# A two-layer hybrid decoder on one core: other slot counts for the experts, 512-column turns for the small ones, whole-piece splits, rows summed ahead of the transposes

## The chip, the core and the metric

The kernel runs on one core of a Trainium2 chip. The core has five engines, each with an instruction queue of its own that it works through in order: PE (TensorE, matrix products; its weight loads are listed as PEld), DVE (VectorE), ACT (ScalarE), POOL (GpSimd) and SP (SyncE, which here issues the transfers). Sixteen DMA engines move data between HBM and the on-chip memory SBUF. Matrix products are written to PSUM, eight banks of 128 x 512 fp32. The metric is the device time of one execution in microseconds; the kernel before takes 1657.78 us (median of three runs, 1655.46 to 1666.21).

## What is computed

Two decoder layers over 256 tokens of 1024 features, all in float32. Each layer has a mixer with three head groups and then a feed-forward part; layer 0 has a dense SwiGLU, layer 1 a top-2-of-8 expert SwiGLU. The change touches the experts alone. Cut to that:

```python
def moe_swiglu(x, w_router, w1, w3, w2):            # w1, w3: 8 x 1024 x 3584; w2: 8 x 3584 x 1024
    xf = x.reshape(-1, D)                           # 256 tokens
    logits = jnp.einsum('nd,de->ne', xf, w_router)
    top_logits, top_idx = lax.top_k(logits, 2)
    gates = jax.nn.softmax(top_logits, axis=-1)
    ...                                             # each token goes to its two experts only
    def expert_block(args):
        xb, e = args
        h = jax.nn.silu(xb @ w1[e]) * (xb @ w3[e])
        return h @ w2[e]
    ...                                             # times the gate, added over the two experts
```

The 256 tokens make 512 assignments. With the reference's default inputs (seed 0) its router gives the eight experts 72, 21, 20, 180, 51, 52, 32 and 84 of them.

## The kernel before

**Precision.** fp32 products are made of fp32r halves: `split(src, hi, lo)` lets ACT copy the source rounded to `hi` (L174) and DVE write the rest, `lo = src - hi` (L175). `mm3` then makes hi x hi, lo x hi and hi x lo, three matmuls for one.

**Weights.** All expert weights are read, 8 x 3 x 14 MiB, in pieces of 1 MiB: 128 partitions x 2048 fp32. `stage` takes a landing buffer `w` and issues the transfer on SP (L186), alternately from the pools "base" and "more"; `parts` takes a `whi` and a `wlo` buffer of the same pool and splits the piece in two halves of 1024 columns. Per pool there are three `w`, two `whi`, two `wlo` (`WB = (3, 2, 2)`), so six landing buffers and four pairs. A `w` is free when DVE has made its `wlo`, a pair when PE has used it.

**Experts.** Routing, up to about 605 us, ranks the tokens. Expert 0 always is job 0 (its first weights are loaded before the routing is known); the other seven are sorted by the number of their tokens and become jobs 1 to 7. A job has a fixed number of slots: 128 for job 0, 256 for job 1, 128 for jobs 2 to 4, 64 for jobs 5 to 7. `gather` picks a job's tokens by one-hot matmuls into `x` (hi and lo), `scatter` brings results back and adds them to `xt`, by gate. If any job has more tokens than slots, a second pass under `tc.If(over > 128)` at the end does the remainder; it is skipped otherwise.

- `one_by_one` does jobs 0, 2, 3, 4, each in NF = 7 steps of 512 hidden columns. In a step `first` makes x @ w1 and x @ w3 with the 128 slots as the stationary operand and 512 weight columns moving (two pieces each, 12 matmuls a piece, `t<-whi,x`), then SiLU and product, four transposes (L1204), `hT` (hi and lo), and `second` for the step before (two pieces of `w2`, 12 matmuls each, `py<-whi,hT`). One step: six pieces.
- `side_by_side` then does job 1 and jobs 5 to 7 together in 14 steps of 256 hidden columns. For job 1, w1 and w3 are stationary and 256 slots move (`t<-x,whi`, two groups `a` of 48 matmuls), `jT` is the result, and `w2` follows a step later. For the small jobs `mm_packed` makes two matmuls of three: the 64 slots' hi and lo stand side by side as 128 stationary columns (`flat(a)`, L1154 and L1158), the `wlo` term uses the 64 hi columns alone (L1156). Three such 256-column turns follow each step of job 1; the two halves of their result are added (`both`, L1279 ACT, L1280 DVE), then SiLU and product for all three turns (L1296, L1297), six transposes of 64 rows (L1261) and a split into `hT`. One step: three pieces of job 1 and nine of the small jobs.

`chores` is a list of gathers and scatters done in small portions between. PSUM holds two banks `t1` and six banks `py`. The order of instructions on each engine is set before the run by a scheduler that starts from the order of the code and follows each operation's inputs and buffers.

Of the kernel before, what the change touches and what calls it, by code (L numbers as in the profile page):

```python
# [7 lines left out]
F32 = mybir.dt.float32  # L8
F32R = mybir.dt.float32r
# [29 lines left out]
def tile_hybrid_decoder(ctx: ExitStack, tc: tile.TileContext, x_in, w_in, mix_scale, w_out, gdn_conv_w,  # L39
# [10 lines left out]
    wp = {"more": None, "small": None, "n": 0,  # L50
# [138 lines left out]
    def parts(staged):  # L189

        which, w = staged
# [757 lines left out]
    def moe(l):  # L949
        li = l // 2  # L950
        with ExitStack() as es:
# [39 lines left out]
            main = [Job(0, 128), Job(1, 256)] + [Job(k, 128 if k < 5 else 64) for k in range(2, NE)]  # L991
# [26 lines left out]
            slots = gp.tile([128, SEQ], F32, name="slots")  # L1018
            G.iota(slots, pattern=[[1, SEQ]], base=1, channel_multiplier=0, allow_small_or_imprecise_dtypes=True)
# [30 lines left out]
            pair = gp.tile([128, 2, 64], F32, name="pair")  # L1050
            V.tensor_copy(pair, slots[:, None, :64].to_broadcast([128, 2, 64]))
            pair = pair.rearrange("p s t -> p (s t)")
# [21 lines left out]
            def gather(jb, tag, pos=posj):  # L1074

                n, k = jb.n, jb.k
                big = n == 256
                w = min(n, 128)
# [4 lines left out]
                for c in range(n // w):  # L1083
                    oh = gp.tile([128, NB, 128], F32R, name="oh", tag="oh", bufs=2)
                    row = pair if n == 64 else slots[:, jb.base + 128 * c:jb.base + 128 * c + 128]
                    for b in range(NB):
                        V.tensor_scalar(oh[:, b, :], row, pos[:, b, k:k + 1], None, op0=OP.is_equal)
# [9 lines left out]
                    for hf in range(2):  # L1097
# [3 lines left out]
                        cut = x[:, 4 * hf:4 * hf + 4, :, w * c:w * c + w]  # L1101
# [113 lines left out]
            def side_by_side(big, small, pend):  # L1215

                n = FFN_EXPERT // 256
                steps = [(jb, f) for jb in small for f in range(n)]
                late = big_late = None
                for f in range(n + 1):  # L1220
                    now = steps[3 * f:3 * f + 3]
                    if f < n:
                        hT = gp.tile([128, 2, 2, SEQ], F32R, name="jT", tag="hT", bufs=4)
# [3 lines left out]
                        for a in range(2):  # L1227
                            p = bank("t1").rearrange("p (m t) -> p m t", m=2)
# [4 lines left out]
                            h = gp.tile([128, SEQ], F32, name="h", tag="h", bufs=2)  # L1233
                            S.activation(h, p[:, 0, :], AF.Silu)
                            V.tensor_mul(h, h, p[:, 1, :])  # L1235
                            split(h, hT[:, a, 0, :], hT[:, a, 1, :])
                    if f == 0:
                        second(*pend)
                        chores.append((pend[0], scatter(pend[0], "py")))
                        chore()  # L1240
                    else:
# [4 lines left out]
                        for g, y in enumerate(big.y):  # L1246
                            t = slice(128 * g, 128 * g + 128)
                            for hf in range(2):
                                cc = slice(512 * hf, 512 * hf + 512)
                                mm3(y[hf], [((big_late[:, k, 0, t], big_late[:, k, 1, t]), (hi[:, k, cc], lo[:, k, cc]))  # L1250
                                            for k in range(2)], f == 1, f == n, True)
                        if f == n:
                            chores.append((big, scatter(big, "t1")))
                            chore()
                    if f < n:
                        big_late = hT
                    if late:
                        hs, before = late
                        pt = bank("t1")[:, :384].rearrange("p (q t) -> p q t", q=6)
                        for q in range(6):  # L1260
                            T.transpose(pt[:, q, :], hs[:, q // 2, 0, 128 * (q % 2):128 * (q % 2) + 128],  # L1261
                                        ident[:64, :64])
                        sT = gp.tile([128, 6, 2, 64], F32R, name="hT", tag="hT", bufs=4)
                        split(pt, sT[:, :, 0, :], sT[:, :, 1, :])
                    if now:
                        both = gp.tile([64, 3, 2, 256], F32, name="both", tag="both", bufs=1)
                    for i in range(3):
                        if now:
                            jb, fs = now[i]
                            if jb.x is None:  # L1270
                                chores.append((jb, gather(jb, "t1")))
                            ws = [load(jb.rows(w)[:, :, 256 * fs:256 * fs + 256], 8, 256) for w in (moe_w1, moe_w3)]
                            finish(jb)
                            p = bank("t1").rearrange("p (m t) -> p m t", m=2)
                            for m, w in enumerate(ws):
# [129 lines left out]
```

## Time and profile before

| | us |
|---|---|
| median of 3 runs (1655.46 to 1666.21) | 1657.78 |
| the profiled execution: its own time | 1654.85 |
| its span in the trace | 1652.6 |
| `one_by_one`, 605 to 1108 | 503 |
| `side_by_side`, 1108 to 1631 | 523 |
| PE, DVE, ACT busy over the span | 1564.1, 1370.0, 1020.7 |
| moved over the span | 430.03 MB |

Busy times of engines overlap. Matmuls are pipelined and their ends are modelled, so a PE that is "busy" may still have room; the distance between starts of consecutive matmuls says more. A wait is put down to the one that ended last. The bounds of the two stages are the first expert matmul, the first of `side_by_side`'s group `a=0`, and the last matmul of the last `w2` piece.

### The profile page before, as it was taken

How to read it: one execution, taken by the hardware profiler on the slowest of the kernel's cores; microseconds unless marked ns; L12 is line 12 of the kernel's file. 1: busy time of each engine (PE TensorE's matmuls, PEld its weight loads, DVE VectorE, ACT ScalarE, POOL GpSimd, SP SyncE). 2: the span in 40 equal slices, each digit the busy share in tenths (PEclk: the TensorE clock that was granted, in tenths of full speed). 3: DMA queues.
4: the chain of work that ended last, by engine and by line, in shares of the span. 5: the costliest groups of instructions: out<-in, count | busy, mean ns of one | idle time of the engine just before them, and what ended most of it. 6: DMA issues, size and time to landing. Idle time of an engine off the chain costs nothing. (4 is left out here: it accounts for less than half of the span.)

```text
span 1652.6 us, 28180 instructions
## 1 busy us (share of the span) xinstructions
PE 1564.1 (95%) x11147; PEld 1358.0 (82%) x11147; DVE 1370.0 (83%) x1902; ACT 1020.7 (62%) x1375; POOL 66.3 (4%) x82
## 2 busy tenths in 40 slices
PE   7898899998899979999999999999999999999995
PEld 6887699996888768888888888888888889888893
DVE  7987854555898788998989889887998988898997
ACT  5334544442425457777777767766787777777783
POOL 5001100000201100000000000000000000000000
PEclk9999899998899979999999999999999999999998
DMA  5351755532314567999999999997999999999991
GB/s 146 104 165 68 228 197 190 176 114 79 91 53 167 178 230 272 363 366 338 362 342 349 331 345 350 333 343 264 355 364 335 343 324 328 366 323 337 344 372 75
DMA packets 274795, 430.03 MB, mean 260 GB/s; under 512 B 11900, under 2 KB 181938, under 8 KB 274656
## 3 DMA queue, kind: packets, MB, share of 16 engines
q1 hardware_dynamic: 272864, 423.81, 74.4%
q0 software_dynamic: 1792, 4.35, 0.9%
q8 instruction: 89, 1.46, 0.4%
q14 instruction: 50, 0.41, 0.1%
HBM read 427.08 MB, written 1.05 MB: 259 GB/s over the span
## 5 line engine op out<-in xcount | busy, mean ns | idle before, releaser
L175 DVE TENSOR_TENSOR wlo<-w,whi 128x1024 fp32r<-128x1024 f32 (+1 forms) x812 | 938.7, 1203 | 133.7 <-ACT whi L174 126.0
L174 ACT ACTIVATE whi<-w 128x1024 fp32r<-128x1024 f32 (+1 forms) x812 | 792.0, 1037 | 227.1 <-PE py L217 43.2
L215 PE MATMUL t<-whi,x 128*128 128x512 f32 x448 | 179.4, 400 | 0.3 <-DVE x L175 0.3
L217 PE MATMUL t<-whi,x 128*128 128x512 f32 x448 | 176.2, 393 | 0.0
L222 PE MATMUL t<-wlo,x 128*128 128x512 f32 x448 | 124.4, 396 | 0.0
L215 PE MATMUL t<-x,whi 128*128 128x256 f32 x448 | 109.5, 282 | 0.0
L219 PE MATMUL t<-x,whi 128*128 128x256 f32 x448 | 109.4, 282 | 0.0
L215 PE MATMUL pj<-xth,whi 128*128 128x256 f32 x368 | 98.4, 302 | 5.7 <-ACT whi L174 2.5
L215 PEld LDWEIGHTS t<-whi,x 128*128 128x128 f32 x448 | 84.2, 188 | 19.9 <-DVE x L175 0.5
L222 PEld LDWEIGHTS t<-wlo,x 128*128 128x128 f32 x448 | 83.8, 188 | 20.1 <-DVE wlo L175 0.4
L217 PEld LDWEIGHTS t<-whi,x 128*128 128x128 f32 x448 | 84.4, 188 | 18.2
L1154 PE MATMUL t<-whi,x 128*128 128x256 f32 x588 | 87.3, 287 | 8.5 <-DVE x L175 3.3
L219 PE MATMUL pj<-xtl,whi 128*128 128x256 f32 x368 | 94.8, 292 | 0.0
L1156 PE MATMUL t<-wlo,x 128*64 128x256 f32 x672 | 94.5, 282 | 0.0
L1154 PEld LDWEIGHTS t<-whi,x 128*128 128x128 f32 x588 | 78.1, 190 | 14.6 <-DVE h L1235 4.4
L215 PE MATMUL py<-whi,hT 128*128 128x512 f32 x224 | 88.0, 393 | 0.0
L217 PE MATMUL py<-whi,hT 128*128 128x512 f32 x224 | 87.4, 390 | 0.0
L219 PE MATMUL ph<-xtl,whi 128*128 128x256 f32 x352 | 86.9, 285 | 0.0
L215 PE MATMUL ph<-xth,whi 128*128 128x256 f32 x352 | 86.8, 284 | 0.0
L219 PEld LDWEIGHTS t<-x,whi 128*128 128x128 f32 x448 | 84.4, 188 | 0.8
L215 PEld LDWEIGHTS t<-x,whi 128*128 128x128 f32 x448 | 84.4, 188 | 0.7
L1156 PEld LDWEIGHTS t<-wlo,x 128*64 128x64 f32 x672 | 81.8, 136 | 1.8
(426 smaller groups left out, 2792.7 us busy)
## 6 DMA issues: line engine op xcount, KB each, us to landing
w<-in_moe_w_dram SPq DMA_DIRECT2D x333, 1024.0 KB, 6.4
w<-in_ffn_w_dram SPq DMA_DIRECT2D x33, 1024.0 KB, 5.3
w<-in_w_in_dram SPq DMA_DIRECT2D x18, 1024.0 KB, 5.5
w<-in_w_out_dram SPq DMA_DIRECT2D x8, 1024.0 KB, 5.1
w<-in_w_in_dram SPq DMA_DIRECT2D x14, 512.0 KB, 3.8
spare<-in_moe_w_dram SPq DMA_DIRECT2D x3, 1024.0 KB, 5.1
xt<-in_x_dram SPq DMA_DIRECT2D x2, 512.0 KB, 4.1
gam<-in_ln_mix_g_dram POOLq DMA_DIRECT2D x2, 512.0 KB, 4.3
```

The source lines that it names most:

```text
L174: S.activation(hi, src, AF.Copy)
L175: return V.tensor_sub(lo, src, hi.bitcast(F32))
L215: T.matmul(o, a[0], b[0], start=first and i == 0, stop=False)
L217: T.matmul(o, a[1], b[0], start=False, stop=False)
L219: T.matmul(o, a[0], b[1], start=False, stop=False)
L222: m = T.matmul(o, a[0], b[1], start=False, stop=last and i == n - 1)
L1154: T.matmul(o, flat(a), b[0], start=first and i == 0, stop=False)
L1156: T.matmul(o[:64], a[:, 0, :], b[1], start=False, stop=False)
```

## The change

Jobs have 128, 192 and 128 slots for jobs 0, 1, 2, and 64 for jobs 3 to 7. `one_by_one` does jobs 0 and 2 only. `side_by_side` runs two generators in turns: `wide` (job 1, 256-column steps as before, but 192 moving slots, and for `w2` three matmuls for its first 128 slots and two, packed, for its last 64) and `packed` (jobs 3 to 7, one after the other, each in 7 steps of 512 columns; a piece of w1 or w3 has 4 x 512 columns like those of `one_by_one`). In `packed` the two halves of a result, each 64 x 512, are added by ACT and DVE as they come; w1's and w3's sums are then transposed separately, and SiLU and product follow on 128 x 256. `wide` yields after `a=0`, after `a=1` and after `w2` (42 times), `packed` once a step (35 times). In the whole expert layer a piece is split in one ACT and one DVE operation of 2048 columns. The second pass, if it is needed, covers all eight jobs.

```diff
     def parts(staged):
 
+        if wp["whole"]:
+            return whole_parts(staged)
         which, w = staged
...
+    def whole_parts(staged):
+        which, w = staged
+        m = w.shape[1] * w.shape[2]
+        r = []
+        for name, n in (("whi", WB[1]), ("wlo", WB[2])):
+            t = wp[which].tile([128, 2048], F32R, name=name, tag=name, bufs=n)
+            r.append(t[:, :m].rearrange("p (a b) -> p a b", a=w.shape[1]))
+        split(w, *r)
+        return r
...
     def moe(l):
         li = l // 2
+        wp["whole"] = True
...
-            main = [Job(0, 128), Job(1, 256)] + [Job(k, 128 if k < 5 else 64) for k in range(2, NE)]
+            main = [Job(0, 128), Job(1, 192), Job(2, 128)] + [Job(k, 64) for k in range(3, NE)]
...
-            slots = gp.tile([128, SEQ], F32, name="slots")
+            slots = gp.tile([128, SEQ + 64], F32, name="slots")
...
-            pair = gp.tile([128, 2, 64], F32, name="pair")
-            V.tensor_copy(pair, slots[:, None, :64].to_broadcast([128, 2, 64]))
...
+            def packed(jobs, tag):
+
+                pend = None
+
+                def half(jb, w, f):
+
+                    p = bank("t1")
+                    for j, src in zip((0, 4), first_pieces(jb, w, f)):
+                        hi, lo = load(*src)
+                        mm_packed(p, [(jb.x[:, j + q], (hi[:, q, :], lo[:, q, :])) for q in range(4)], j == 0, j == 4)
+                    r = gp.tile([64, 512], F32, name="both", tag="both", bufs=3)
+                    S.activation(r, p[64:], AF.Copy)
+                    V.tensor_add(r, r, p[:64])
+                    return r
+
+                def close(jb, sT, f):
+                    if f == 0:
+                        jb.y = [jb.ys()]
+                    for q, src in zip((0, 2), second_pieces(jb, f)):
+                        hi, lo = load(*src)
+                        for hf in range(2):
+                            cc = slice(512 * hf, 512 * hf + 512)
+                            mm_packed(jb.y[0][hf], [(sT[:, q + k], (hi[:, k, cc], lo[:, k, cc])) for k in range(2)],
+                                      f == 0 and q == 0, f == NF - 1 and q == 2)
...
+                for n, jb in enumerate(jobs):
...
+                    for f in range(NF):
+                        if f == 0:
+                            finish(jb)
+                        hs = [half(jb, moe_w1, f)]
+                        yield
+                        hs.append(half(jb, moe_w3, f))
+                        if pend:
+                            close(*pend)
+                        chore()
+
+                        pt = bank("t1").rearrange("p (m q t) -> p m q t", m=2, q=4)
+                        for m, r in enumerate(hs):
+                            for q in range(4):
+                                T.transpose(pt[:, m, q, :], r[:, 128 * q:128 * q + 128], ident[:64, :64])
+                        h = gp.tile([128, 4, 64], F32, name="h", tag="h", bufs=2)
+                        S.activation(h, pt[:, 0], AF.Silu)
+                        V.tensor_mul(h, h, pt[:, 1])
+                        sT = gp.tile([128, 4, 2, 64], F32R, name="sT", tag="hT", bufs=4)
+                        split(h, sT[:, :, 0, :], sT[:, :, 1, :])
+                        pend = (jb, sT, f)
...
+            def wide(big):
...
+                n, nt = FFN_EXPERT // 256, big.n
+                before = None
                 for f in range(n + 1):
                     if f < n:
+                        hT = gp.tile([128, 2, 2 * nt], F32R, name="jT", tag="hT", bufs=4)
                         ws = [load(big.rows(w)[:, :, 256 * f:256 * f + 256], 8, 256) for w in (moe_w1, moe_w3)]
...
                         for a in range(2):
+                            p = bank("t1")[:, :2 * nt].rearrange("p (m t) -> p m t", m=2)
...
+                            yield
+                    if f > 0:
...
                         hi, lo = load(big.rows(moe_w2)[:, 2 * f - 2:2 * f, :], 2, D)
+                        for hf in range(2):
+                            cc = slice(512 * hf, 512 * hf + 512)
+                            ws = [(hi[:, k, cc], lo[:, k, cc]) for k in range(2)]
+                            mm3(big.y[0][hf], [((before[:, k, :128], before[:, k, 256:]), ws[k]) for k in range(2)],
+                                f == 1, f == n, True)
+                            mm_packed(big.y[1][hf], [(before[:, k, 128:256].rearrange("p (s t) -> p s t", s=2), ws[k])
+                                                     for k in range(2)], f == 1, f == n)
...
+                        yield
                     if f < n:
+                        before = hT
+
+            def side_by_side(big, small, pend):
+
+                a, b = wide(big), packed(small, "t1")
+                na, nb = 3 * (FFN_EXPERT // 256), NF * len(small)
+                done = 0
+                next(a)
+                second(*pend)
...
+                for i, _ in enumerate(b):
+                    while (done + 1) * nb < (i + 1) * na and next(a, "end") != "end":
+                        done += 1
+                for _ in a:
+                    pass
                 chore(100)
...
-            pend = one_by_one([main[k] for k in (0, 2, 3, 4)], [main[1], main[5]])
-            side_by_side(main[1], main[5:], pend)
+            pend = one_by_one([main[k] for k in (0, 2)], [main[1], main[3]])
+            side_by_side(main[1], main[3:], pend)
...
-                pend = one_by_one([Job(k, 128, 128) for k in (0, 2, 3)] + [Job(k, 128, 64) for k in (5, 6, 7)])
+                pend = one_by_one([Job(k, 128, 192 if k == 1 else 128 if k < 3 else 64) for k in range(NE)])
```

Three places show what the change does to the queues. The first is PE, two pieces of w1 of a small job before; `t1` is the PSUM bank, `whi` and `wlo` the weight buffers, `x` the packed slots (numbers tell buffers apart).

```order
L1154 MATMUL t1_12102<-whi_12088,x_10952 128x256 x7
L1156 MATMUL t1_12102<-wlo_12089,x_10952 64x256 x8
L1158 MATMUL t1_12102<-whi_12088,x_10952 128x256
L1154 MATMUL t1_12102<-whi_12096,x_10952 128x256 x7
L1156 MATMUL t1_12102<-wlo_12097,x_10952 64x256 x8
L1158 MATMUL t1_12102<-whi_12096,x_10952 128x256
```

Here the same place now, two pieces of w3 of a small job.

```order
L1167 MATMUL t1_11278<-whi_11281,x_10843 128x512 x3
L1169 MATMUL t1_11278<-wlo_11282,x_10843 64x512 x4
L1171 MATMUL t1_11278<-whi_11281,x_10843 128x512
L1167 MATMUL t1_11278<-whi_11295,x_10843 128x512 x3
L1169 MATMUL t1_11278<-wlo_11296,x_10843 64x512 x4
L1171 MATMUL t1_11278<-whi_11295,x_10843 128x512
```

A piece has moved from 16 matmuls of 256 columns to 8 of 512, and both pieces now belong to one of the two matrices.

The second place is DVE in the middle of `side_by_side` before, from the product of job 1's group `a=0` on; `w` is the landing buffer, `jT` and `hT` the transposed hidden values.

```order
L1235 TENSOR_TENSOR h_12766<-h_12766,t1_12717 128x256
L175 TENSOR_TENSOR wlo_12879<-w_12876,whi_12878 128x1024 x2
L175 TENSOR_TENSOR jT_12700<-h_12766,jT_12700 128x256
L175 TENSOR_TENSOR wlo_12922<-w_12919,whi_12921 128x2x512 x2
L1235 TENSOR_TENSOR h_12820<-h_12820,t1_12771 128x256
L175 TENSOR_TENSOR jT_12700<-h_12820,jT_12700 128x256
```

And ACT now, from the two first pieces of a step of job 1 (`whi_11213`, `whi_11219`) over the six packed pieces that stand between its groups `a=0` (`t1_11223`) and `a=1`; the last of the six, `whi_11384`, follows four rows later.

```order
L174 ACTIVATE whi_11213<-w_11211 128x2048
L174 ACTIVATE whi_11219<-w_11217 128x2048
L1274 ACTIVATE h_11164<-t1_11155 128x256
L174 ACTIVATE sT_11167<-h_11164 128x4x64
L174 ACTIVATE whi_11281<-w_11279 128x2048
L1239 ACTIVATE both_11207<-t1_11175 64x512
L174 ACTIVATE whi_11295<-w_11293 128x2048
L1304 ACTIVATE h_11272<-t1_11223 128x192
L1307 ACTIVATE jT_11210<-h_11272 128x192
L174 ACTIVATE whi_11312<-w_11310 128x2048
L1239 ACTIVATE both_11307<-t1_11278 64x512
L174 ACTIVATE whi_11326<-w_11324 128x2048
```

Before, a piece was two rows of 1024 columns, and between job 1's two products stood its own splits, the last pieces of a small job and the coming `w2`; now a piece is one row of 2048, and a small job's next pieces stand between job 1's two groups.

The third place is PE at the end of those six pieces, where `a=1` begins (`t1_11399`), on the buffers that `a=0` used.

```order
L1167 MATMUL t1_11367<-whi_11384,x_10843 128x512 x3
L1169 MATMUL t1_11367<-wlo_11385,x_10843 64x512 x4
L1171 MATMUL t1_11367<-whi_11384,x_10843 128x512
L227 MATMUL t1_11399<-x_8193,whi_11213 128x192
L231 MATMUL t1_11399<-x_8193,whi_11213 128x192
```

The second use of `whi_11213` stands behind six packed pieces, where the groups of job 1 followed each other before.

## Rows read from the trace of the kernel before

**Rows 1.** The page, part 1: busy time, share of the span, instructions of each engine.

```profile
PE 1564.1 (95%) x11147; PEld 1358.0 (82%) x11147; DVE 1370.0 (83%) x1902; ACT 1020.7 (62%) x1375; POOL 66.3 (4%) x82
```

**Rows 2.** Busy time by stretch; the columns stand in the first line.

```profile
core 0: us, PE busy (x) PEld busy (x) DVE busy (x) ACT busy (x) POOL busy (x), PEclk, DMA share, GB/s
605.00:1108.00 503.00, 501.29 (x2277) 409.41 (x2278) 445.39 (x443) 368.98 (x415) 0.00 (x0) 1.00 0.94 339
1108.00:1631.00 523.00, 506.77 (x3496) 451.34 (x3496) 464.36 (x494) 392.35 (x481) 1.10 (x2) 0.99 0.96 329
700.00:1080.00 380.00, 380.00 (x1710) 309.75 (x1709) 334.73 (x328) 277.63 (x315) 0.00 (x0) 1.00 0.96 347
1140.00:1600.00 460.00, 448.61 (x3140) 401.46 (x3140) 410.23 (x432) 348.00 (x424) 1.10 (x2) 1.00 1.00 341
```

**Rows 3.** Waits from 700 to 1100 us: total, times, longest; ACT's, then SP's.

```profile
ACT whi L174 <- PE t L217: 24.7, 35, 2.4
...
SPq L186 <- DVE wlo L175: 316.5, 131, 5.2
```

**Rows 4.** Timeline of ACT in stage A: start, length, what.

```profile
690.97 0.58 ACT L174 ACTIVATE hT<-t 128x512 fp32r<-128x512 f32 x1
...
708.02 0.58 ACT L174 ACTIVATE hT<-t 128x512 fp32r<-128x512 f32 x1
```

**Rows 5.** Timeline of PE: start, length (of xN: of the whole run), what.

```profile
801.39 1.03 PE L1100 MATMUL py<-ident,xs 128*128 128x128 f32 x8
...
1104.84 0.28 PE L215 MATMUL t<-x,whi 128*128 128x256 f32 x1
1104.96 0.28 PE L219 MATMUL t<-x,whi 128*128 128x256 f32 x1
...
1113.63 0.40 PE L217 MATMUL py<-whi,hT 128*128 128x512 f32 x1
1113.86 0.40 PE L215 MATMUL py<-whi,hT 128*128 128x512 f32 x1
...
1302.14 0.58 PE L1261 MATMUL t<-ident,both 64*128 64x64 f32 x6
...
1309.19 1.10 PE L1156 MATMUL t<-wlo,x 128*64 128x256 f32 x8
```

**Rows 6.** Groups by line and form, 720 to 1652: busy, mean ns, idle before.

```profile
L175 DVE TENSOR_TENSOR wlo<-w,whi 128x1024 fp32r<-128x1024 f32 x590 | 687.2, 1215 | 69.8 <-ACT whi L174 64.0 <-PE t L224 5.4
L174 ACT ACTIVATE whi<-w 128x1024 fp32r<-128x1024 f32 x588 | 579.8, 1051 | 106.7 <-PE t L219 24.3 <-PE t L217 21.6 <-PE t L1158 21.0
...
L1280 DVE TENSOR_TENSOR both<-both,t 64x512 f32<-64x512 f32 x42 | 28.2, 672 | 0.4 <-ACT both L1279 0.4
...
L175 DVE TENSOR_TENSOR hT<-t,hT 128x512 fp32r<-128x512 f32 x22 | 15.0, 683 | 2.5 <-ACT hT L174 2.5
...
L1204 PE MATMUL t<-ident,h 128*128 128x128 f32 x88 | 13.2, 272 | 0.0
...
L175 DVE TENSOR_TENSOR jT<-h,jT 128x256 fp32r<-128x256 f32 x28 | 11.7, 418 | 3.9 <-ACT jT L174 3.9
```

**Rows 7.** Busy time in two stretches of 10 us; columns as in rows 2.

```profile
610.00:620.00 10.00, 8.34 (x39) 6.53 (x38) 10.00 (x14) 8.28 (x9) 0.00 (x0) 1.00 1.02 394
...
1220.00:1230.00 10.00, 10.00 (x74) 9.14 (x74) 8.15 (x10) 7.93 (x11) 0.00 (x0) 1.00 1.07 368
```

**Rows 8.** Timeline of DVE in `side_by_side`: start, length of the run, what.

```profile
1308.86 6.89 DVE L175 TENSOR_TENSOR wlo<-w,whi 128x1024 fp32r<-128x1024 f32 x6
```

**Rows 9.** Stretches of 2 us where `side_by_side` begins; columns as in rows 2.

```profile
1124.00:1126.00 2.00, 0.00 (x0) 0.00 (x0) 2.00 (x4) 0.00 (x0) 0.00 (x0) 0.79 0.28 107
1126.00:1128.00 2.00, 1.78 (x8) 1.78 (x9) 0.17 (x1) 0.00 (x0) 0.00 (x0) 0.50 0.49 132
...
1130.00:1132.00 2.00, 2.00 (x12) 2.00 (x11) 1.72 (x2) 1.19 (x2) 0.00 (x0) 0.51 0.07 23
```

**Rows 10.** Timeline of PE there: start, length, what, idle before and its releaser.

```profile
1126.22 1.01 PE L1154 MATMUL t<-whi,x 128*128 128x256 f32 x3 [2.90 <-DVE x L175]
```

More of the change, by code (lines that the diff above doesn't have):

```diff
@@ L48, in tile_hybrid_decoder @@
     mcst = mixers.enter_context(tc.tile_pool(name="mcst", bufs=1, reuse_waits="tile"))
-    wp = {"more": None, "small": None, "n": 0,
+    wp = {"more": None, "small": None, "n": 0, "whole": False,
           "base": ctx.enter_context(tc.tile_pool(name="wgt", bufs=1, side="right", reuse_waits="tile"))}
@@ L1082, in gather @@
                 jb.ohT = []
[L1083 removed]
+                for c in range(0, n, 128):
+                    w = min(n - c, 128)
                     oh = gp.tile([128, NB, 128], F32R, name="oh", tag="oh", bufs=2)
[L1085 removed]
                     for b in range(NB):
[L1087 removed]
+                        dst, row = oh[:, b, :], slots[:, jb.base + c:jb.base + c + w]
+                        if w == 64:
+                            dst, row = dst.rearrange("p (s t) -> p s t", s=2), row[:, None, :].to_broadcast([128, 2, 64])
+                        V.tensor_scalar(dst, row, pos[:, b, k:k + 1], None, op0=OP.is_equal)
                     xs = [gp.tile([128, 512], F32, name="xs", tag="h", bufs=2) for hf in range(2)]
@@ L1212, in one_by_one @@
                 return pend
[L1215 to L1219, printed above, removed]
+            def packed(jobs, tag):
[18 more added lines that the diff above has]
+                                      f == 0 and q == 0, f == NF - 1 and q == 2)
+                    if f == NF - 1:
+                        chores.append((jb, scatter(jb, tag)))
+                        chore()
+                for n, jb in enumerate(jobs):
+                    if jb.x is None:
+                        chores.append((jb, gather(jb, tag)))
+                    for f in range(NF):
[6 more added lines that the diff above has]
+                            close(*pend)
+                        chore()
+                        pt = bank("t1").rearrange("p (m q t) -> p m q t", m=2, q=4)
[8 more added lines that the diff above has]
+                        pend = (jb, sT, f)
+                        if f == NF - 3 and n + 1 < len(jobs):
+                            chores.append((jobs[n + 1], gather(jobs[n + 1], tag)))
+                        chore()
+                close(*pend)
@@ L1295, in side_by_side @@
-                    if now:
-                        S.activation(both[:, :, 0, :], both[:, :, 0, :], AF.Silu)
-                        V.tensor_mul(both[:, :, 0, :], both[:, :, 0, :], both[:, :, 1, :])
-                        late = (both, now)
-                        for jb, _ in steps[3 * f + 3:3 * f + 9]:
-                            if jb.x is None and not any(jb is c[0] for c in chores):
-                                chores.append((jb, gather(jb, "t1")))
+                        before = hT
```

73 lines of the change are left out of this document (13 added, 60 removed).

## The prediction

> **What bounds the kernel now.** The page first [rows 1]: TensorE is busy 95% of the span, VectorE 83%, so averages settle nothing and the expert layer has to be read by stage. It has two [rows 2]: A, `one_by_one` (605 to 1108 us, four experts of 128 slots, 28 steps of 512 hidden columns), and B, `side_by_side` (1108 to 1631, 14 steps, each one big and three small 256-column steps). Weights come in pieces of 1 MiB, 168 per stage; ACT makes `whi`, DVE `wlo`, PE uses both.
>
> In stage A the waits [rows 3] show ACT waiting for PE to give `whi` buffers back and SP waiting for DVE to free a landing buffer; no engine waits for a transfer. One step, from one `hT` to the next without gather or scatter, takes 708.02 - 690.97 = 17.05 us [rows 4]. PE's starts stand 0.23 us apart with 512 columns and 0.12 with 256 [rows 5]; 72 matmuls x 0.23 plus four transposes are 17.0. So A is exactly PE. In B a step needs 192 x 0.117 + 48 x 0.23 + 0.6 = 34.1 us of PE (0.117 = (1.10 - 0.28) / 7, the run of eight); 14 steps are 477, with 25 for gathers and scatters 502 of the 523 us. B is PE-bound to 96%, with the transfers close behind: share 1.07 at 368 GB/s in a dense spell [rows 7].
>
> **The change part by part.** The sum is made against the profiled execution's 1654.85 us (span 1652.6 and 2.2 around it), 0.2% under the median of the runs.
>
> *Two experts leave stage A.* 14 of 28 steps go, 14 x 17.05 = 239 us, with half of the 503 - 477 = 26 us for gathers and scatters: A loses 251 and keeps 252.
>
> *Stage B becomes 252 pieces*: 35 packed steps (five experts of 64 slots x 7, six pieces each) and 14 wide steps (192 slots, three pieces). I sum it per resource, for none is hidden behind the others by a margin.
>
> PE. A packed piece is 8 matmuls of 512 columns instead of 12: 1.84 us. A packed step is 6 x 1.84 + 0.7 (eight 64-column transposes; six last 0.58) = 11.7; 35 are 411. A wide step has 96 matmuls of 192 columns and 20 of 512. No row has 192 columns. Scaled from 256 they would take 0.088; if loading 128 weight columns sets the pace they stay at 0.117; a run of eight 128-column transposes, 0.27 us each [rows 6], has (1.03 - 0.27) / 7 = 0.108, though only half as many columns move, so I take 0.11. A wide step is then 10.6 + 4.6 = 15.2 (13.0 to 15.8), 14 are 212 (182 to 221). With 30 for gathers and scatters PE needs 653 (623 to 662).
>
> DVE. A split of 1024 columns lasts 1.215 us, one of 512 0.683 [rows 6]: 1.04 ns a column, so 2.28 for 2048. Queued, a run of six takes 6.89 [rows 8], so each overlaps its neighbour by 0.08: two halves 2.29, a whole piece 2.21. 252 pieces are 557. The rest, by the same rows less 0.07 each: 35 x 1.9 for a packed step (two adds, one product, one subtraction), 14 x 1.3 for a wide one, 34 for scatters and gathers: 119. DVE needs 676; in stage B before it was busy 464 of 523, 89% [rows 2].
>
> Transfers. 252 pieces are 264.2 MB. Stage A's plain step moves 6.29 MB in 17.05 us, 369 GB/s, with 512- and 1024-column rows, which most of B now also has. At that rate B takes 716 us. Bounds: 394, a dense stretch of 10 us [rows 7], 671; 347 and 341, the averages of most of A and of B with their stops [rows 2], 761 and 775. The Trainium skill (DMA: Bandwidth & Descriptors, "Where 436 GB/s comes from") says that the HBM side binds a load from HBM at about 358 GB/s. By that B would take 738, a step of A 17.6, and the sum would be 1627. The trace does not agree: A holds 369.
>
> ACT needs less: 1.051 for 1024 columns [rows 6], so about 1.9 for 2048, 252 x 1.9 + 125 = 604.
>
> *A wait the change adds.* There are four `whi`/`wlo` pairs, two per pool. A wide step now takes its two first pieces, does `a=0`, then one packed step (six pieces) stands in PE's queue ahead of `a=1`, which still needs both. So six pieces pass through two pairs. One pair's round is 1.9 (ACT) + 2.28 (DVE) + 1.15 (the five matmuls after `wlo` arrives) + 0.1 = 5.4 us, 2.7 per piece, where DVE alone would need 2.2: 3.0 us over six pieces. During `a=0` and `a=1` (5.3 us each) DVE can fill only two pairs, 4.4: 2 us more. While DVE waits, its adds and products behind the blocked `wlo` wait too, and PE for them. Before, with halves, DVE could start after 1.05, a round was 4.6, and no other expert's first pieces stood between the two groups. DVE's other work fills part of the 5 us: 0 to 5 us x 14, so DVE with holds is 676 to 746; I take the middle, 711.
>
> Transfers (716) and DVE (711) are thus equally high and share six landing buffers, so what one loses the other cannot make up. Stage B before ran 4% over its highest sum (523 against 502); I take 2.5% over 716: **735**.
>
> *Nothing*: the wider `slots` on POOL and one DVE operation more against two `pair` copies ahead of the routing are under 1 us. The repeat pass under `over > 128` is not entered: the reference's router, on its default inputs, gives the experts 72, 21, 20, 180, 51, 52, 32 and 84 assignments, which fit 128 / 192 / 128 / 64. What follows 1631 us (last scatter, LayerNorm) stays.
>
> Sum: 1654.85 - 251 - 523 + 735 = **1616 us**; in general 881 + B.
>
> **The rivals.**
> 1. *PE was all that held it.* For: no engine of A waits for a transfer, and 394 GB/s occurs. Then B runs at 675 to 695 (transfers at 380 to 391, just under the 394), 1556 to 1576. Against: that asks DVE's 676 us with hardly any idle time, and it was busy 89% in either stage [rows 2].
> 2. *The held pairs decide.* For: two of four pairs are out for some 27 us in every wide step, and 89% was all DVE reached in B before; 676 / 0.89 = 760, and transfers at 341 to 347 give 761 to 775. 1641 to 1656: no change that can be measured. Against: in A, where nothing was held, DVE was not asked for more.
> 3. *TensorE's clock falls, and it is slower.* At 1123 us PE waited 2.90 us for DVE [rows 10], and from 1126 to 1132 the granted clock was 0.50, the lower of its two levels, 1.2 of 2.4 GHz [rows 9]: about 6 us at half speed, 3 us lost and the wait besides. The Trainium skill (TensorE: Matmul & The Clock Gate, "HAM oscillation — how this bites in real kernels") tells of gaps between bursts that return the clock to half each time; this row agrees. PE will now idle about 80 of 735 us. My held spell has gaps of 1.2 to 1.5 us, half of that row's. If they grow to it, each fall makes the next pieces late: 28 spells x (3 + 1.5) = 126 us at most. It decides from some 18 falls on (B above 791, 1672 and more); with all, 1730.
>
> That the work is not saved at all is excluded by the order: the packed rows have two matmuls per weight block where `one_by_one` had three.
>
> **How the numbers follow.** This kernel's measurement can tell about 1% (17 us) from no change, that is B below 760 or above 793. Forecast (B 700 to 760): 0.61. Rival 1: 0.12. Rival 2: 0.18. Rival 3: 0.09. So faster 0.73, same 0.18, slower 0.09. The time is the forecast's, 1616; its own range is 1581 to 1641. The range given, 1578 to 1652, adds most of rival 2 and leaves out rival 1 (most of 0.12) and rival 3.
>
> **What would show it.** A's plain step still 17.05 us, and A ending near 857. B with PE waiting for `wlo` and `whi` in 1 to 1.5 us pieces, between 192-column groups above all; DVE over 91% busy; 350 to 370 GB/s. `wlo` rows 128x2048 near 2.28 us. The 192-column pitch 0.09 to 0.117. I am wrong if PE is still over 96% packed by pitch in B (then its price is off), if B's transfers exceed 385 GB/s (rival 1), if they fall under 345 with landing buffers waiting for held pairs (rival 2), or if the granted clock in B is under 0.97 (rival 3).

## The result: 4% slower

The changed kernel takes 1726.12 us (median of four runs, 1724.76 to 1729.08), the kernel before, beside it, 1657.65. The ratio is 1.0416, with a 95% interval of 1.0395 to 1.0437. The forecast was 1616, with a range that ended at 1652.

The profile of the changed kernel, the two stages first (columns as in [rows 2]):

```profile
608.00:858.00 250.00, 247.67 (x1106) 200.70 (x1107) 212.91 (x140) 176.37 (x124) 0.00 (x0) 0.99 0.92 328
858.00:1703.00 845.00, 730.60 (x3747) 538.52 (x3746) 677.01 (x535) 564.41 (x484) 1.10 (x2) 0.93 0.86 309
```

Stage A lasts 250 us (252 forecast). Stage B lasts 845 instead of 735: the whole error of 110 us lies there. Against [rows 2] no engine is fuller than it was: PE is busy 86%, DVE 80%, and the transfers fell from a share of 0.96 to 0.86. The granted clock fell from 0.99 to 0.93.

The costliest groups of DVE and PE in stage B (line, engine, operation, form, count | busy, mean ns | idle before, with its releasers):

```profile
L175 DVE TENSOR_TENSOR wlo<-w,whi 128x2048 fp32r<-128x2048 f32 x252 | 571.2, 2284 | 135.2 <-ACT whi L174 133.3 <-PE t L236 1.1
L1240 DVE TENSOR_TENSOR both<-both,t 64x512 f32<-64x512 f32 x70 | 47.1, 673 | 0.5 <-ACT both L1239 0.5
L1275 DVE TENSOR_TENSOR h<-h,t 128x256 f32<-128x256 f32 x35 | 14.3, 409 | 0.0
L231 PE MATMUL t<-x,whi 128*128 128x192 f32 x448 | 108.5, 282 | 0.0
```

The prices of the operations were right: a whole split takes 2.284 us (2.28 taken), DVE's work adds up to 677 us (676). With the starts of this trace (512 columns 0.23 us apart, 192 columns 0.111) PE's instructions of stage B come to 649 us (653). So 649 of 845 us are work at full speed, and nearly 200 are something else. What PE waited for in stage B (tile and line that waited, what ended the wait: total, times, longest):

```profile
PE t L1167 <- DVE h L1275: 22.4, 11, 4.3
PE py L1169 <- DVE wlo L175: 21.5, 19, 1.6
PE t L1167 <- DVE xt L1142: 7.7, 2, 3.9
PE py L1167 <- DVE sT L175: 7.5, 4, 2.1
PE t L227 <- DVE h L1275: 6.8, 3, 2.5
PE t L1140 <- DVE xt L1142: 6.6, 3, 3.1
PE t L1140 <- DVE h L1275: 5.3, 2, 2.6
...
PE t L1169 <- DVE wlo L175: 4.6, 7, 0.9
```

All waits are 114 us; in stage B before they were 16 [rows 2]. The product `h` (L1275, 34.5) ends more of them than the splits `wlo` (27), and none of PE's waits ends with a transfer. Of the 22 waits of 2 us and more, nine end with this product, twelve with other short work on DVE (adds, small splits, gathers, scatters), one with ACT and none with `wlo`. The product is 0.41 us long and DVE never idled ahead of it: it stood in a queue. One such place, around 1172 us, on DVE, on PE, on ACT, and by stretches:

```profile
1168.17 0.67 DVE L1240 TENSOR_TENSOR both<-both,t 64x512 f32<-64x512 f32 x1
1168.76 6.68 DVE L175 TENSOR_TENSOR wlo<-w,whi 128x2048 fp32r<-128x2048 f32 x3
1175.37 0.40 DVE L1275 TENSOR_TENSOR h<-h,t 128x256 f32<-128x256 f32 x1
1175.70 0.41 DVE L175 TENSOR_TENSOR x<-t,x 128x256 fp32r<-128x256 f32 x1
1176.26 0.43 DVE L175 TENSOR_TENSOR sT<-h,sT 128x256 fp32r<-128x256 f32 x1
1181.36 2.29 DVE L175 TENSOR_TENSOR wlo<-w,whi 128x2048 fp32r<-128x2048 f32 x1 [4.68 <-ACT whi L174]
```

```profile
1171.04 0.71 PE L1272 MATMUL t<-ident,both 64*128 64x64 f32 x8
1171.58 0.41 PE L1113 MATMUL t<-ident,xs 64*128 64x64 f32 x4
1175.83 1.65 PE L1167 MATMUL t<-whi,x 128*128 128x512 f32 x3 [3.83 <-DVE h L1275]
...
1179.22 0.87 PE L1167 MATMUL t<-whi,x 128*128 128x512 f32 x3
```

```profile
1172.97 0.36 ACT L1274 ACTIVATE h<-t 128x256 f32<-128x256 f32 x1
...
1179.41 1.92 ACT L174 ACTIVATE whi<-w 128x2048 fp32r<-128x2048 f32 x1 [3.19 <-PE t L1171]
```

```profile
1172.00:1174.00 2.00, 0.00 (x0) 0.00 (x0) 2.00 (x2) 1.60 (x3) 0.00 (x0) 1.00 1.02 388
...
1176.00:1178.00 2.00, 2.00 (x5) 1.33 (x6) 0.54 (x2) 0.22 (x1) 0.00 (x0) 0.50 1.05 389
...
1180.00:1182.00 2.00, 2.00 (x10) 1.35 (x9) 0.64 (x1) 1.98 (x3) 0.00 (x0) 1.00 1.09 348
```

Read together: PE writes the transposes of a packed step into one `t1` bank (L1272) and those of a gather into the other (L1113). ACT has its SiLU done at 1173.3, but DVE is in three whole splits in a row, 6.68 us, and the product, which gives the bank back, starts only at 1175.37. PE has both banks taken and stands 3.83 us. Then it starts at half the clock (0.50 granted; three matmuls in 1.65 us, 0.87 three microseconds later). Its first pieces' buffers return late, so ACT cannot write the next `whi` for 3.19 us, and DVE, which had been the one that was waited for, idles 4.68. DVE and PE take turns where they should overlap. The Trainium skill says as much of the queue (PSUM — Partial Sum Buffer, "Engine vs sequencer instructions": the queues of ScalarE, VectorE and GpSimd are strictly first in, first out); the trace agrees, with a 0.40 us product behind 6.68 us of splits.

The place is the rule. In DVE's order 2.4 whole pieces stand on average between the second add of a packed step and its product; in 17 of 35 steps it is three. The product starts over 1 us after its SiLU has ended in 32 of 35 steps, and 16 times PE stands for it. In stretches of 2 us, stage B has 25 separate spells with a granted clock under 0.9, which together make 123 us at 1.2 GHz; half of that, some 61 us, is lost at most (an estimate). In the sum: 649 at full speed, 114 of waits, about 61 of clock, and 21 left over (a kernel below that hardly ever falls has 24), together 845.

### The profile page after: what moved, and what is told of

It reads as the page before. It is cut to its first block, busy times and chain, and to the rows that moved or that the text cites. A ratio compares the mean times of both kernels' runs of the same rounds, so it can differ in the third digit from the quotient of the medians.

```text
span 1723.6 us, 25757 instructions
## 1 busy us (share of the span) xinstructions
PE 1532.9 (89%) x10223; PEld 1235.7 (72%) x10223; DVE 1349.6 (78%) x1636; ACT 999.1 (58%) x1081; POOL 66.4 (4%) x82
## 5 line engine op out<-in xcount | busy, mean ns | idle before, releaser
L175 DVE TENSOR_TENSOR wlo<-w,whi 128x2048 fp32r<-128x2048 f32 (+2 forms) x479 | 918.8, 1939 | 227.6 <-ACT whi L174 223.7
L174 ACT ACTIVATE whi<-w 128x2048 fp32r<-128x2048 f32 (+2 forms) x479 | 765.7, 1625 | 310.9 <-PE t L1171 64.6
L1169 PE MATMUL t<-wlo,x 128*64 128x512 f32 x560 | 163.6, 417 | 4.6 <-DVE wlo L175 4.6
L1167 PEld LDWEIGHTS t<-whi,x 128*128 128x128 f32 x420 | 82.8, 208 | 62.2 <-DVE h L1275 26.3
L1169 PE MATMUL py<-wlo,sT 128*64 128x512 f32 x280 | 95.3, 424 | 21.7 <-DVE wlo L175 21.5
L227 PE MATMUL t<-x,whi 128*128 128x192 f32 x448 | 108.4, 284 | 6.8 <-DVE h L1275 6.8
L231 PE MATMUL t<-x,whi 128*128 128x192 f32 x448 | 108.5, 282 | 0.0
L227 PEld LDWEIGHTS pj<-xth,whi 128*128 128x128 f32 x368 | 72.7, 198 | 12.1 <-ACT whi L174 4.3
L231 PEld LDWEIGHTS pj<-xtl,whi 128*128 128x128 f32 x368 | 72.7, 198 | 0.8 <-issue 0.6
L231 PEld LDWEIGHTS ph<-xtl,whi 128*128 128x128 f32 x352 | 67.4, 192 | 0.6 <-DVE xtl L264 0.2
L227 PEld LDWEIGHTS ph<-xth,whi 128*128 128x128 f32 x352 | 67.5, 192 | 0.4
```

Source lines behind the costliest of these rows:

```text
L174: S.activation(hi, src, AF.Copy)
L175: return V.tensor_sub(lo, src, hi.bitcast(F32))
L227: T.matmul(o, a[0], b[0], start=first and i == 0, stop=False)
L231: T.matmul(o, a[0], b[1], start=False, stop=False)
L1167: T.matmul(o, flat(a), b[0], start=first and i == 0, stop=False)
L1169: T.matmul(o[:64], a[:, 0, :], b[1], start=False, stop=False)
```

## The experiments

All times are medians of four runs. In the table, "B" is stage B by its stretch in the trace, "busy" PE's busy time in it; what is over 649 us of busy time (692 in the kernels with the sum on PE, below) is in part matmuls at the lower clock (about 61 of 82 us in the changed kernel, 9 of 48 in four_banks); the rest, 12 to 50 us by run, isn't explained. "Falls" counts the spells of stage B with a granted clock under 0.9 in stretches of 2 us.

| kernel | us | ratio to before, 95% | B | busy | wait | clock in B | falls |
|---|---|---|---|---|---|---|---|
| before_whole | 1679.5 | 1.0131 to 1.0165 | 549 | 516 | 33 | 0.99 | 2 |
| changed kernel | 1726.1 | 1.0395 to 1.0437 | 845 | 731 | 114 | 0.93 | 25 |
| halves | 1664.7 | 1.0033 to 1.0067 | 790 | 717 | 73 | 0.95 | 15 |
| no_hold | 1691.6 | 1.0196 to 1.0230 | 816 | 712 | 104 | 0.94 | 17 |
| four_banks | 1637.0 | 0.9870 to 0.9903 | 760 | 697 | 63 | 0.99 | 4 |
| act_pool | 1673.8 | 1.0091 to 1.0147 | 796 | 708 | 88 | 0.96 | 13 |
| halves_gate | 1675.1 | 1.0082 to 1.0140 | 798 | 721 | 77 | 0.96 | 15 |
| halves_four_banks | 1617.5 | 0.9736 to 0.9777 | 741 | 704 | 37 | 0.99 | 3 |
| halves_u_only | 1626.6 | 0.9794 to 0.9840 | 751 | 706 | 45 | 0.98 | 9 |
| halves_sum_only | 1635.8 | 0.9842 to 0.9895 | 762 | 725 | 38 | 0.98 | 9 |
| halves_sum_on_pe | 1611.1 | 0.9715 to 0.9748 | 737 | 716 | 21 | 1.00 | 1 |
| whole_sum_on_pe | 1643.5 | 0.9899 to 0.9949 | 763 | 720 | 43 | 0.99 | 6 |
| halves_sum_no_hold | 1613.5 | 0.9718 to 0.9764 | 739 | 715 | 24 | 0.99 | 2 |
| whole_sum_no_hold | 1637.1 | 0.9843 to 0.9902 | 762 | 724 | 38 | 0.98 | 5 |

The theories at the start: **theory 1**, short DVE operations stand behind runs of splits and PE waits for them through two `t1` banks; **theory 2**, the pairs that job 1 holds (the prediction's own term) make the splits late.

### Halves again (halves)

```diff
-        wp["whole"] = True
+        wp["whole"] = False
```

> The changed kernel (1726.1 us), but every expert piece is split in two halves of 1024 columns again. Its stage B lasts 845 us (858 to 1703), of which TensorE waits 114 and loses 70 more at the lower clock. Theory 1 (small DVE operations stand behind a run of piece splits): the order that the scheduler makes has 4.8 half pieces of wlo between the last add of a packed step and its product, 4.9 before, so little changes: 1695 to 1735. Theory 2 (whole pieces make a pair's round too long, 5.4 us against 4.6, while two pairs are held): 14 x 3 us of waits and as much of clock come back, 1640 to 1680.

61 us came back, within theory 2's numbers and against theory 1's. But not theory 2's waits alone:

```profile
PE t L1167 <- DVE h L1275: 11.6, 10, 3.5
...
PE t L1169 <- DVE wlo L175: 2.7, 6, 0.5
```

PE's waits for `wlo` went from 27 to 4 us, and those for `h`, in all rows, from 34.5 to 17.6, although as many columns of splits stand ahead of the product as before. Its waits of 2 us and more went from nine to two, yet it still starts 2.0 us behind its SiLU on average (2.5 in the changed kernel). Why so little less halves PE's wait isn't shown.

### No held pairs (no_hold)

```diff
                                 V.tensor_sub(hT[:, a, o:o + t.stop - t.start], h[:, t], hi[:, t].bitcast(F32))
-                            yield
+                            if a == 1:
+                                yield
...
-                na, nb = 3 * (FFN_EXPERT // 256), NF * len(small)
+                na, nb = 2 * (FFN_EXPERT // 256), NF * len(small)
```

> The changed kernel without the turn between job 1's groups a=0 and a=1, so that no packed pieces stand between them and no pair is held over six of them. Theory 2 (held pairs): 14 x 5 us of waits go and the clock's losses with them, 1600 to 1660. Theory 1 (product behind piece splits): the order has 5.7 half pieces between add and product instead of 4.9, so no gain: 1715 to 1760.

Between the two ranges: 35 us faster than the changed kernel. The waits of stage B say how:

```profile
PE t L1167 <- DVE h L1275: 26.9, 8, 6.1
...
PE py L1169 <- DVE wlo L175: 6.1, 7, 1.4
```

The waits for `wlo` went from 27 to 8 us, so held pairs were real. The product's grew (44.5 in all rows, from 34.5; the longest is 6.1), with more splits ahead of it. Each theory owns a part.

### Four banks (four_banks, and with halves: halves_four_banks)

```diff
...
-                return ps.tile([128, 512], F32, name=tag, tag=tag, bufs={"t1": 2, "py": 6}[tag])
+                return ps.tile([128, 512], F32, name=tag, tag=tag, bufs={"t1": 4, "py": 4}[tag])
...
-                            big.y = [big.ys() for g in range(2)]
+                            big.y = [big.ys()] * 2
...
```

Both kernels leave out the separate sums of job 1's first 128 and last 64 slots: both go into the same two `py` banks, so that part of the result is changed. The instructions are as many and as large as before.

> The changed kernel with four t1 banks in place of two: both halves of job 1's result are summed into the same two py banks (that part of the result is changed, the number and size of all instructions are not), which leaves four py banks. Theory 1, with the two t1 banks as the place where TensorE waits for the product: the waits on h, xt, x and both (62 of 114 us) mostly go, and about half of the 70 us of clock: 1620 to 1665. Theory 2 (held pairs) and a theory that DVE's order alone decides, wherever TensorE waits: no gain, 1705 to 1735.

> The changed kernel in halves and with four t1 banks (job 1's two halves summed into the same two py banks: that part of the result is changed, the instructions are not). A limit for what waits cost. If nothing but TensorE's waits for DVE held stage B, its 790 us lose the 51 us of waits through t1 banks and some 40 us of clock, down to the transfers at stage A's rate of 369 GB/s (716): 1570 to 1600. If transfers already hold it at the 353 GB/s that the run with four banks and whole pieces has from 900 to 1600 us, stage B takes about 748: 1615 to 1635.

The first loses 89 us with DVE's work unchanged, within theory 1's numbers: PE's waits for `h`, `xt`, `x` and `both` are gone from its list, and the falls are 4 instead of 25. So the two banks are where DVE's queue reached PE. Its stage B (in the trace of a run of 1631.0 us; columns as in [rows 2]):

```profile
850.00:1610.00 760.00, 697.10 (x3755) 511.79 (x3754) 674.97 (x538) 561.54 (x483) 1.10 (x2) 0.99 0.95 343
```

Of the 63 us of waits that were left, 44.6 ended with `wlo`:

```profile
PE py L1169 <- DVE wlo L175: 30.9, 31, 1.6
PE t L1169 <- DVE wlo L175: 11.9, 20, 1.4
```

With halves these are 19 us and the kernel takes 1617.5, in the second range: stage B does not come down to 716 even with banks to spare. That range was put on transfers at 353 GB/s; from 880 to 1560 us they moved 364.

### The product off DVE (act_pool)

```diff
+                        u = gp.tile([128, 4, 64], F32, name="u", tag="both", bufs=3)
+                        S.activation(u, pt[:, 1], AF.Copy)
-                        V.tensor_mul(h, h, pt[:, 1])
+                        G.tensor_mul(h, h, u)
-                        split(h, sT[:, :, 0, :], sT[:, :, 1, :])
+                        S.activation(sT[:, :, 0, :], h, AF.Copy)
+                        G.tensor_sub(sT[:, :, 1, :], h, sT[:, :, 0, :].bitcast(F32))
```

> The changed kernel, but in a packed step ACT also copies the w3 half of the transposes out of PSUM (128x256, about 0.4 us, 35 times), and POOL makes the product and the subtraction of sT: DVE has no part in what gives the transposes' bank back. Theory 1: TensorE's waits for the product and for sT (44 of 114 us) and their share of the clock's 70 us go, unless POOL takes more than 2 us an operation: 1640 to 1685. Theory 2 (held pairs): 1710 to 1735.

52 us faster, in the slower half of theory 1's range: a part of the waits moved to the copy, since ACT too has whole pieces in its queue, and to `wlo`.

```profile
PE py L1169 <- DVE wlo L175: 29.8, 28, 1.5
PE t L1167 <- ACT u L1276: 8.9, 6, 2.1
```

### An order forced on DVE (halves_gate)

```diff
+            def behind():
+                return after("prod") if "prod" in marks else nullcontext()
...
-                        hi, lo = load(*src)
+                        with behind() if j else nullcontext():
+                            hi, lo = load(*src)
...
-                        V.tensor_mul(h, h, pt[:, 1])
+                        marks["prod"] = V.tensor_mul(h, h, pt[:, 1])
```

and `with behind():` around job 1's loads. `after("prod")` makes the operations of a load follow the marked product in the queues.

> The changed kernel in halves (1664.7) with an order forced on DVE: the splits of a packed step's second piece, and of job 1's pieces, stand behind the product of the packed step before; the order has 1.7 half pieces of wlo between the last add and the product instead of 4.8. If DVE's order is what makes TensorE wait, the waits for h and sT (23 of 72 us in stage B) go with some 20 of the 59 us at the lower clock: 1615 to 1645. If the splits that are put behind come too late in their turn, waits for wlo (3.8 us now) take their place: 1655 to 1690.

10 us slower than halves, in the second range, but not for its reason: the waits for `wlo` went only from 4 to 10 us. The product's waits fell from 17.6 to 10.4, but the adds took their place, 27 us after 4.5:

```profile
PE t L1167 <- DVE both L1244: 16.5, 9, 2.1
PE t L1276 <- DVE both L1244: 10.4, 5, 2.4
PE t L1167 <- DVE h L1279: 9.3, 7, 2.2
```

Splits that no longer stand ahead of the product stand ahead of the adds. What the best order would give isn't shown by this one; the next runs take short operations on which banks depend out of DVE's queue.

### DVE out of the banks' way (halves_sum_on_pe, and its two edits apart)

Edit u, and edit sum; `id2` is two 64 x 64 identities on top of each other, so a matmul with it transposes and adds the rows of hi and lo.

```diff
+                        u = gp.tile([128, 4, 64], F32, name="u", tag="both", bufs=3)
+                        S.activation(u, pt[:, 1], AF.Copy)
-                        V.tensor_mul(h, h, pt[:, 1])
+                        V.tensor_mul(h, h, u)
```

```diff
-                    r = gp.tile([64, 512], F32, name="both", tag="both", bufs=3)
-                    S.activation(r, p[64:], AF.Copy)
-                    V.tensor_add(r, r, p[:64])
+                    r = gp.tile([128, 512], F32, name="both", tag="both", bufs=3)
+                    S.activation(r, p, AF.Copy)
...
-                                T.transpose(pt[:, m, q, :], r[:, 128 * q:128 * q + 128], ident[:64, :64])
+                                T.matmul(pt[:, m, q, :], r[:, 128 * q:128 * q + 128], id2, start=True, stop=True)
```

> The changed kernel in halves (1664.7), with DVE out of what gives the t1 banks of a packed step back: ACT copies the whole 128x512 result to SBUF, the transposes become matmuls with two identities on top of each other and so add the hi and lo rows (280 matmuls of 64 columns instead of transposes), and ACT copies the w3 half out of PSUM ahead of the product. DVE has 70 adds of 0.67 us (47 us) less, ACT 14 us more. If the waits for the product and for the adds are the cause (h 18 and both 5 of the 72 us, and their share of 59 us of clock): 1610 to 1640. If the banks that gathers and scatters hold (xt, x, ohT, xs: 29 us) weigh as much: 1635 to 1660. If ACT, whose order these copies then stand in, becomes what TensorE waits for: above 1660.

> The changed kernel in halves (1664.7) with only one of the two edits of halves_sum_on_pe (1611.1): ACT copies the w3 half of the transposes to SBUF, so that the product no longer holds a t1 bank; DVE's adds stay. If the product behind piece splits is the main wait (18 us and its share of the clock's 59): 1625 to 1640. If it is the adds, which hold the bank of the result and come ahead of everything in a step: 1650 to 1668.

> The other of the two edits alone: the hi and lo rows are summed by TensorE in the transposes, DVE has no adds, the product still reads the transposes' bank. If the adds are the main cause (47 us of DVE, and the result's bank given back by ACT alone): 1615 to 1630. If the product is: 1640 to 1660.

From halves, u alone gives 38 us, in the range for the product as the main wait. Sum alone gives 29; its 1635.8 falls between its two ranges. Both give 54, in the first range, less than the two gains added. Both together make the fastest kernel of the study, 2.7% under the kernel before and 6.7% under the changed one. Stage B of it, and the core of it:

```profile
851.00:1588.00 737.00, 716.15 (x4037) 554.33 (x4036) 651.99 (x717) 583.58 (x769) 1.10 (x2) 1.00 0.97 354
880.00:1560.00 680.00, 662.25 (x3743) 513.26 (x3743) 604.96 (x662) 543.71 (x716) 1.10 (x2) 1.00 1.00 365
```

The clock is granted in full, PE waits 21 us in all, and the transfers have a share of 1.00 at 365 GB/s over 680 us. The waits that are largest in total are now these:

```profile
PE t L1172 <- DVE wlo L175: 4.6, 11, 0.5
PE t L1170 <- ACT both L1242: 3.9, 5, 1.0
```

The sum on PE isn't free. A step's eight transposes, 0.71 us, become 16 records that take 1.89 us together:

```profile
1023.07 1.89 PE L1274 MATMUL t<-id,both 128*128 128x64 f32 x16
```

35 times 1.2 us is some 42 us more of PE (692 instead of 649 by its starts), and the kernel is faster all the same.

### Whole pieces and held pairs with that mended (whole_sum_on_pe, whole_sum_no_hold, halves_sum_no_hold)

The edits are those above, with and without `wp["whole"]`.

> Both edits of halves_sum_on_pe, with whole-piece splits as in the changed kernel. If whole pieces hurt only through the short DVE operations that stand behind them, they cost little here, 5 us in stage A and 5 to 10 in B: 1615 to 1630. If the longer round of the pairs, with two of them held, costs by itself (27 us of waits for wlo in the changed kernel, 4 with halves, and the clock's share): 1640 to 1670.

> whole_sum_on_pe (1643.5) without the turn between job 1's groups a=0 and a=1. Whole pieces cost 32 us against halves_sum_on_pe (1611.1), and TensorE waits 21 us for wlo there against 6. If that is the pairs that job 1 holds over six packed pieces, the waits for wlo go and with them most of the 32 us: 1612 to 1628. If it is the whole piece as such, an own round of 5.4 us in place of 4.6 and short operations behind 2.28 us in place of 1.2, in whatever order: 1636 to 1652. In halves the same edit gave nothing (1613.5 against 1611.1).

> halves_sum_on_pe (1611.1) without the turn between job 1's groups. Its stage B takes 737 us with the transfers at 358 GB/s and a share of 0.98. If transfers hold it now, nothing comes of it: 1603 to 1619. If held pairs still cost (TensorE waits 20 us in all there, 6 of them for wlo): 1585 to 1602.

Whole pieces still cost 32 us (1643.5 against 1611.1), now by `wlo` coming late, as PE's largest waits in whole_sum_on_pe show:

```profile
PE py L1172 <- DVE wlo L175: 12.2, 18, 1.6
PE t L1172 <- DVE wlo L175: 8.9, 11, 1.4
```

Taking the held pairs away gives 6 of these 32 us, and in halves nothing. Both kernels with whole pieces lie in their second range, that with halves in its first. So with these short operations out of the way the whole piece as such costs, and the held pairs hardly count. Whether it costs by its longer round, or by what still stands behind it, isn't told apart. The held pairs counted (35 us) where the short operations stood in DVE's queue.

### Whole pieces in the kernel before (before_whole)

```diff
     def parts(staged):
...
+        if wp["whole"]:
+            split(w, *r)
+            return r
...
     def moe(l):
...
+        wp["whole"] = True
```

> The kernel before with the one edit that every expert piece is split whole, 2048 columns at once. Halves gave the changed kernel 62 us back. If whole pieces cost that much only where other experts' pieces stand between and TensorE waits for short DVE work (stage B of the changed kernel), then here stage A loses some 8 us (4 for 14 steps in the changed kernel) and stage B little: 1657 to 1672. If they cost by themselves, by longer rounds of the four pairs in any order, stage B loses 25 to 60 us and TensorE's clock falls there: 1685 to 1725.

Between the two ranges, 23 us slower than the kernel before. By stage:

```profile
606.00:1107.00 501.00, 497.70 (x2229) 404.39 (x2228) 428.23 (x272) 349.90 (x247) 0.00 (x0) 1.00 0.94 337
1107.00:1656.00 549.00, 516.21 (x3548) 457.95 (x3547) 458.42 (x332) 384.43 (x319) 1.10 (x2) 0.99 0.93 316
```

Nothing in stage A against [rows 2]; 26 us in stage B. PE's waits in it rise from 16 to 33 us, and the clock stays at 0.99. So whole pieces cost something without a turn between job 1's groups and with two falls of the clock only.

## Why the prediction was wrong

**Right.** Two experts out of stage A: 252 us left, 250 measured. PE's price 653 (649), the 192-column matmuls at 0.11 us (0.111), a whole split 2.28 us, DVE's work 676 (677). ACT's 604 was too high (564).

**Right by luck.** The held pairs were priced at 35 us of DVE's time, and no_hold gave 35 us of the kernel's. DVE's time did not hold the stage, though, and with the short operations out of DVE's queue the same edit gives 6 us or nothing.

**The step that failed** is the last of stage B's sum: "Stage B before ran 4% over its highest sum (523 against 502); I take 2.5% over 716". The 4% came from a stage in which PE was the bound, busy 507 of 523 us; it was taken over to one in which three engines pass a bank and four pairs around. There 845 us came out of a highest sum of 716. The prediction added busy times by engine, and asked of DVE only how much work it has, not where in its queue the product stands. It wrote that adds and products would wait behind a blocked `wlo`, "and PE for them", but only inside the held spell, 0 to 5 us a wide step. The product waits in nearly every packed step (over 1 us in 32 of 35), behind splits that run one after the other, and PE waits because two `t1` banks carry results, transposes, gathers and scatters: two more banks alone give 89 us back. The orders that were shown ahead of the prediction gave a hint of it: on DVE before, and on ACT now, short operations stand between splits. The changed kernel's order on DVE was not among them.

**Its transfers term was never reached** in the changed kernel: 309 GB/s, share 0.86. In halves_sum_on_pe, with the waits mended, 365 GB/s holds for 680 us, and stage B takes 737 us. That is the forecast's number, yet no proof of its working, since PE's price there is 692. The Trainium skill's 358 GB/s for a load from HBM (DMA: Bandwidth & Descriptors, "Where 436 GB/s comes from") is passed by 2% there, over 680 us.

**The clock rival** had the sign and nearly the size, and its own sign came: the clock is under 0.97 (0.93). It priced a fall at 4.5 us; there were 25, and 25 x 4.5 = 113 over 735 make 848 for the 845 measured. In part that is luck. By the rows a fall cost some 2.5 us of clock (61 / 25), and PE idled 32 us more than the 82 that 735 holds beyond 653, which is 1.3 us a fall; the rest is what was left over above. The cause was another, too: the rival had the gaps of the held spell grow. They did not (the longest wait for `wlo` is 1.6 us), while nine waits for the product were 2.1 to 4.3. It got 9 in 100 because only those gaps, of 1.2 to 1.5 us, were looked at. Its sums don't agree with each other either: at 4.5 us a fall, 791 is passed at 13 falls, not 18, and 28 falls make 735 + 126 + 881 = 1742, not 1730. What the Trainium skill tells of gaps between bursts (TensorE: Matmul & The Clock Gate, "HAM oscillation — how this bites in real kernels") is what this stage does, 25 times; there the gaps are waits for transfers, here for DVE. No run changed the clock alone, so its 61 us are read from the rows and not tested apart. The falls went with the long waits more than with all of them: the changed kernel, halves, four_banks and halves_sum_on_pe have 22, 12, 4 and no waits of 2 us and more, and 25, 15, 4 and 1 falls.

**The whole splits** were priced as a gain for DVE (2.21 for 2.29 us). Halves cost DVE 13 us more (690 against 677 busy in stage B) and make the kernel 61 us faster.

Two things stay open: why the product's wait halves with half pieces though as much work stands ahead of it, and whether transfers or PE hold the last 737 us. From 880 to 1560 us of halves_sum_on_pe, ACT waits 3.8 us for transfers and 42 us for PE to give `whi` back. That speaks for PE, but no run changed either alone.

## What to carry to other kernels

When a kernel moves from one full engine to several nearly full ones, a sum of busy times is a lower bound only; look in each in-order queue for the short operation that gives a PSUM bank back, and count what stands ahead of it. Let that bank be released by an engine with less in its queue, here by a copy on ACT, and try long streaming operations in pieces, even if the pieces cost more in sum. Here a long stall of TensorE was paid twice, once as the wait and once at the lower clock after it: halves waits 73 us with 15 falls, four_banks 63 us in shorter waits with 4.

## What was not expected of the hardware

POOL was slow at short work: in act_pool a product of 128x256 from SBUF took 2.8 us and the subtraction 1.5 us (0.41 and 0.42 on DVE). PE waited only 0.7 us for them in all; `sT` is used a step later.

```profile
L1277 POOL TENSOR_TENSOR h<-h,u 128x256 f32<-128x256 f32 x35 | 98.2, 2805 | 844.7 <-ACT u L1276 844.7
L1280 POOL TENSOR_TENSOR sT<-h,sT 128x256 fp32r<-128x256 f32 x35 | 52.3, 1495 | 58.5 <-ACT sT L1279 58.5
```

Matmuls of 192 columns start (1.06 - 0.28) / 7 = 0.111 us apart in the changed kernel, those of 256 columns 0.117 to 0.12 [rows 5]: a quarter fewer columns save little more than one twentieth.

```profile
882.23 1.06 PE L236 MATMUL t<-x,wlo 128*128 128x192 f32 x8
```
